# Hybrid attention and state-space layer on one core: one large load behind each of six combining steps on GpSimd, combining weights asked for five units sooner, the last gate applied to the sum

## The chip, the cores and the metric

The kernel runs on one core of a Trainium2 chip. The metric is device time in microseconds (us): the median of several executions for the kernel before, and one further execution recorded by the hardware profiler. Engines are written as in the profile: PE (TensorE matmul), PEld (its weight load), DVE (VectorE), ACT (ScalarE), POOL (GpSimd), SP (SyncE, which here only issues DMAs).

## The reference, cut to what matters

One decoder layer of 2048 tokens and width 1024. Three attention results with different dilations are merged by a softmax over their log-sum-exps, gated and normalised; a state-space branch is computed beside it; both go through one output projection and a layer norm.

```python
o1, l1 = dilated_window_attention(q, k, v, slopes, 1)
o2, l2 = dilated_window_attention(q, k, v, slopes, 4)
o3, l3 = dilated_window_attention(q, k, v, slopes, 16)
wts = softmax(stack([l1, l2, l3]), axis=0)
y_att = wts[0]*o1 + wts[1]*o2 + wts[2]*o3
y_att = rms_norm(y_att * silu(z_att), att_norm_g)
...
mix = concatenate([y_att, y_ssm])
out = mix @ w_out
x = layer_norm(alpha * x + out, ln_g, ln_b)
```

## The kernel before, in words

Up to about 1235 us of the span the kernel computes the input projection, the convolution and the state-space branch. That part is not touched. The change lies in the attention (1235 to 1727 us) and in the output projection (from 1727 us on).

**Attention.** The 16 heads are handled as 8 pairs (`pr` 0 to 7). A pair has 24 units, named by `(d, qd, half)`: three dilations `d`, four groups `qd`, two halves. Here `d` 0, 1, 2 is the dilation 16, 4, 1. The loop index `i` runs over all 192 units and three stages are in flight: at index `i` PE does the scores of unit `i`, the transposes of unit `i-2` (`TA = 2`) and the products with the values of unit `i-3`. The engines PE, DVE, ACT and POOL execute in exactly the order in which the code is written; only SP's order is chosen by the framework's scheduler. A condition such as `at == (1, 3, 0)` is tested with the unit whose values were just done, so what it guards stands three scores behind.

For a pair the tiles `q` and `k` (1 MB each, two alternating sets, so that the next pair's can be loaded while this pair runs), one `v` and, for `d` 1 and 2, a shifted `vs` (about 1 MB each) and a table `tb` per dilation are loaded. POOL issues the loads of `q`, `k`, `v`, `vs` and of the output weights `W`; it issues them in its program order, between its arithmetic. POOL also writes two permuted copies of `q` (`permute`, tile `ex`).

After a pair's last unit, `statistics(…, 1)` transposes the maxima and sums of the softmax on PE (L886), ACT copies them, SP stores them to DRAM (`d_st`), and `gather` (L906) loads them back in another layout as `cm`. Two calls of `weights` (L908) work out the three merging weights on DVE and ACT and store them (`d_wd`, L924).

**Combining.** While the next pair runs, `combine` forms the pair's merged and gated output on POOL. Each of its first three steps loads a 1 MB tile `wb`, which repeats rows of `d_wd` over 64 partitions (L937, two DMAs of 512 KB on SP), and multiplies the dilation's result `num` with it (L939); the second and third add the sum so far (L948). A fourth step multiplies by the gate `z_att` (L954) and stores the result to `d_ua` (L955). There are three `wb` slots, so the three tiles are asked for at once.

**Order before.** In the pair that runs, `weights` stands behind units `(1,1,0)` and `(1,1,1)`, the four combining steps behind `(1,3,0)`, `(2,0,0)`, `(2,1,1)`, `(2,3,0)`. `q` and `k` of the next pair are asked for at `(0,1,0)`, this pair's `v`, `vs` of `d` 2 at `(0,3,0)`, the next pair's `v` of `d` 0 at `(1,0,0)`, its `v`, `vs` of `d` 1 at `(2,1,0)`.

**Output projection.** 64 items of 24 matmuls: 16 row blocks by two branches by two halves of the columns. The first eight items use the state-space branch of four row blocks, so that the attention's last pair can be combined meanwhile, on DVE. For the last pair the gate is applied to each of the three `num` tiles beforehand (`gate`, L1071, one on POOL, two on DVE), and the third combining step writes the sum into four `PT` tiles. `split` and `squares` prepare a block, `add` merges an item into the row, `scaled` scales the residual, `norm` ends a row block.

Of the kernel before, what the change touches and what calls it, by code (L numbers as in the profile page):

```python
# [28 lines left out]
def hybrid_layer(ctx, tc, xT, xc, w52, wv, convw, convb, dtb, alog, dskp, gcol, wout,  # L29
# [669 lines left out]
    with ExitStack() as c2:  # L699
# [16 lines left out]
        def load_qk(A):  # L716
            pr = A["pr"]
            for x, src in (("q", d_q), ("k", d_k)):
                t = qk[pr % 2].tile([128, NR, NJ], F32, name=x)
                nc.gpsimd.dma_start(f2(t), src[pr])  # L720
                A[x] = {0: t} if x == "q" else t

        def load_dil(A, d):
# [5 lines left out]
            for x, o in (("v", 0),) if d == 0 else (("v", 0), ("vs", 1)):  # L729
                t = A[x][d] = io.tile([128, 16, 128], F32, name=x, bufs=3)  # L730
                if d == 0:
                    for j in range(4):
                        nc.gpsimd.dma_start(t[j:128:4], dap(d_v[0], j * D + pr * 128,
                                                            [[64 * D, 32], [4 * D, 16], [1, 128]]))
                else:
                    nc.gpsimd.dma_start(t[:, 0:16 - o], dap(d_v[d % 2], 64 * o * D + pr * 128,
                                                            [[D, 128], [128 * D, 16 - o], [1, 128]]))
# [188 lines left out]
        def combine(A, d):  # L926
# [6 lines left out]
            acc = A.get("acc")  # L933
            if d < 3:
                wb = cm_.tile([128, NR, NJ], F32, name="wb", bufs=3)
# [4 lines left out]
                if d == 2 and last:  # L940
                    for i in range(4):
                        u7.append(io.tile([128, 2, 2, 128], F32, name="PT", bufs=4).rearrange("p a b t -> p (a b) t"))
                        o7 = u7[i].rearrange("p n (r j) -> p r n j", j=8)
                        eng.tensor_tensor(o7, pv(wb)[:, :, 4 * i:4 * i + 4], pv(acc)[:, :, 4 * i:4 * i + 4],
                                          op=OP.add)
                    return
                if d:
                    eng.tensor_tensor(wb, wb, acc, op=OP.add)  # L948
                A["acc"] = wb
                return  # L950
            zt = cm_.tile([128, NR, NJ], F32, name="wb", bufs=3)
            nc.sync.dma_start(f2(zt), d_za[pr])
            u = f2(cm_.tile([128, NR, NJ], F32, name="wb", bufs=3))
            eng.tensor_tensor(pu(u), pv(acc), pv(zt), op=OP.mult)  # L954
            nc.sync.dma_start(dap(d_ua, pr * 128, [[7 * 128, 128], [128 * 7 * 128, 16], [1, 128]]),  # L955
                              u.rearrange("p (n t) -> p n t", t=128))
# [10 lines left out]
        def load_w(e, hf, name=None):  # L967
# [3 lines left out]
            s = slice(hf * 512, hf * 512 + 512)  # L971
# [97 lines left out]
        def gate(d, eng):  # L1069
            num = f2(pairs[7]["num"][d])  # L1070
            eng.tensor_tensor(num, num, zt7, op=OP.mult)  # L1071

        O = {}
        pairs = {}
        LOADS = [(8, 0, "k_0", (0, 0, 1)), (9, 0, "q_0", (0, 1, 0)), (10, 0, "ex", (0, 1, 1)), (11, 0, "vs", (0, 2, 0)),
# [7 lines left out]
        with tc.manual_schedule(engines={E.PE, E.DVE, E.Activation, E.Pool}):  # L1083
            for i in range(len(todo) + TA + 1):
                if i < len(todo):
                    pr, d, qd, half = todo[i]
                    if i == 0:
                        pairs[0] = load_pair(0)
                        load_qk(pairs[0])
                        for k in range(3):  # L1090
                            load_dil(pairs[0], k)
# [3 lines left out]
                    if (d, qd, half) == (2, 0, 0) and pr < 7:  # L1095
                        permute(pairs[pr + 1], 1)
# [6 lines left out]
                if i > TA:  # L1103
# [15 lines left out]
                    if at == (0, 1, 0) and pr < 7:  # L1119
                        load_qk(pairs[pr + 1])  # L1120
                    if pr and at == (0, 3, 0):
                        load_dil(pairs[pr], 2)
                    if pr < 7:
                        if at == (1, 0, 0):
                            load_dil(pairs[pr + 1], 0)
                        if at == (2, 1, 0):
# [146 lines left out]
```

## Time and profile before

| | us |
|---|---|
| median of 3 runs | 2137.01 |
| range of these | 2133.23 to 2138.12 |
| profiled execution, its own time | 2129.59 |
| its span in the trace | 2127.8 |
| mean granted TensorE clock | 0.969 |

The profile page gives busy time by engine and the costliest groups; the views of the trace used below are the time line of one engine (start, duration, engine, line, tiles, and in brackets the idle time before with what ended it), the chain of work that ended last, the waits, and the busy time in chosen windows. A line `SPq` is a DMA issue on SP, not the transfer. "issue" in the chain is time in which an engine waited for nothing that the trace shows.

### The profile page before, as it was taken

Reading aid. Unit: us, or ns where it says so; the run is one execution under the profiler, and the core shown is the slowest. Engines: PE = TensorE matmul, PEld = TensorE weight load, DVE = VectorE, ACT = ScalarE, POOL = GpSimd, SP = SyncE. Lnnn points to the kernel's source line nnn. Section 1 sums busy time; section 2 is a strip of 40 time slices with the busy share of each in tenths; the row PEclk is TensorE's granted clock in tenths of the full one; section 3 lists DMA queues with packets and bytes.
Section 4 is the critical chain, followed back from the end, with each engine's and each line's share of the span. In section 5 each row is a group of like instructions: output and inputs, shape, how many; then the busy total and the mean of one; then the engine's idle time right before and its main releaser. Section 6 shows DMA issues by size and latency. Waiting matters only on the chain.

```text
span 2127.8 us, 43190 instructions
## 1 busy us (share of the span) xinstructions
PE 1998.0 (94%) x16128; PEld 1626.3 (76%) x16128; DVE 1287.2 (60%) x3077; ACT 1107.9 (52%) x3045; POOL 1062.2 (50%) x877
## 2 busy tenths in 40 slices
PE   8999989989999999989999999999999868999998
PEld 7999768768777788868888867666667646888886
DVE  3441465459898556654444468777778746565453
ACT  4231445435554566646666578888788732222221
POOL 2113446657577566765555432765556771333221
PEclk9999999989999999989999999999999978999999
DMA  9999778966658777898887764777787797432310
GB/s 309 330 352 357 240 231 284 312 251 212 188 185 263 279 247 255 273 399 265 257 257 245 252 240 159 205 198 237 210 238 225 223 322 209 144 116 77 106 67 30
DMA packets 255953, 491.98 MB, mean 231 GB/s; under 512 B 43200, under 2 KB 122176, under 8 KB 244096
## 3 DMA queue, kind: packets, MB, share of 16 engines
q1 hardware_dynamic: 172096, 237.54, 35.7%
q0 software_dynamic: 40304, 168.57, 22.7%
q10 hardware_dynamic: 43344, 83.12, 12.4%
q8 instruction: 127, 2.08, 0.4%
q14 instruction: 82, 0.67, 0.1%
HBM read 333.57 MB, written 163.97 MB: 234 GB/s over the span
## 4 chain that ended last, share of the span: by engine, by line
PE 49%; DMA 7%; ACT 4%; DVE 4%; issue 2%; POOL 1%; SPq 0%; ACTq 0%; POOLq 0%; DVEq 0%
PE pp L302 6%; PE pp L306 6%; PE pp L304 6%; PE N L848 4%; PE S L1027 4%; PE S L1029 4%; PE S L795 4%; PE S L1028 3%; ACT P L807 3%; PE T L822 2%; PE T L1027 2%; PE T L1029 2%; PE T L1028 2%; DVE P L801 1%; DMA wb<-d_wd 1%
## 5 line engine op out<-in xcount | busy, mean ns | idle before, releaser
L258 POOL TENSOR_TENSOR w<-wr,w 128x512 fp32r<-128x512 f32 x231 | 345.2, 1513 | 191.7 <-ACT w L257 149.0
L807 ACT ACTIVATE P<-P,st 128x192 f32<-128x192 f32 (+1 forms) x768 | 322.0, 421 | 71.4 <-DVE st L801 67.0
L801 DVE CUSTOM_DVE_ANT_0 P<-S,tb 128x192 f32<-128x192 f32 (+1 forms) x768 | 206.9, 324 | 104.4 <-PE S L795 82.2
L311 ACT COPY ev<-pp 128x512 f32<-128x512 f32 x176 | 102.7, 583 | 249.6 <-PE pp L306 204.6
L319 DVE TENSOR_TENSOR ev<-pp,ev 128x512 f32<-128x512 f32 x152 | 101.0, 684 | 114.1 <-PE pp L306 80.9
L257 ACT CAST w<-wr 128x512 fp32r<-128x512 f32 x231 | 137.8, 618 | 40.6 <-DVE wr L250 25.4
L939 POOL TENSOR_TENSOR wb<-num,wb 128x2048 f32<-128x2048 f32 x21 | 95.5, 4549 | 125.4 <-DMA wb<-d_wd 72.2
L250 DVE TENSOR_TENSOR wr<-wr 128x512 f32<-128x512 f32 x132 | 139.6, 1058 | 11.8 <-DMA wr<-w 7.6
L807 ACT ACTIVATION_READ_ACCUMULATOR P<-P,st 128x1 f32 x768 | 144.3, 188 | 0.0
L822 PE MATMUL T<-ident,P 128*128 128x128 f32 x768 | 129.2, 291 | 10.5 <-DVE PT L824 7.4
L824 DVE COPY PT<-T 128x512 f32<-128x512 f32 x192 | 131.7, 686 | 5.6 <-PE T L822 5.3
L848 PE MATMUL N<-PT,v 128*64 128x64 f32 (+1 forms) x1536 | 126.7, 262 | 7.8 <-ACT num L878 4.4
L822 PEld LDWEIGHTS T<-ident,P 128*128 128x128 f32 x768 | 82.9, 143 | 56.8 <-issue 21.2
L402 DVE SCALAR_TENSOR_TENSOR acc<-U,cw,acc 128x2048 f32<-128x2048 f32 x36 | 122.6, 3406 | 3.6 <-ACT acc L399 3.2
L795 PE MATMUL S<-k,ex 64*64 64x192 f32 (+1 forms) x2048 | 110.9, 327 | 5.3 <-issue 5.3
L848 PEld LDWEIGHTS N<-PT,v 128*64 128x64 f32 x1536 | 79.4, 138 | 45.7 <-issue 18.7
L147 PE MATMUL pp<-vh,xh 128*128 128x256 f32 (+1 forms) x320 | 91.4, 290 | 11.5 <-ACT xh L165 10.9
L140 POOL TENSOR_TENSOR vl<-vraw,vh 128x256 fp32r<-128x256 f32 (+1 forms) x32 | 29.9, 937 | 129.0 <-ACT vh L139 121.9
L148 PE MATMUL pp<-vl,xh 128*128 128x256 f32 (+1 forms) x320 | 91.2, 289 | 0.0
L1003 DVE TENSOR_REDUCE tb<-P 128x128 f32<-128x1024 f32 x30 | 60.1, 2004 | 46.0 <-ACT P L1000 23.7
L302 PE MATMUL pp<-TT3h,w 128*128 128x512 f32 x176 | 72.7, 413 | 15.0 <-ACT ev L311 14.7
L1065 POOL TENSOR_TENSOR k<-k,wb 128x1024 f32<-128x1024 f32 x8 | 25.8, 3222 | 121.4 <-DVE k L1064 121.4
(440 smaller groups left out, 6130.7 us busy)
## 6 DMA issues: line engine op xcount, KB each, us to landing
wr<-w ACTq DMA_DIRECT2D x157, 256.0 KB
wb<-d_wd SPq DMA_DIRECT2D x48, 512.0 KB
d_wc<-w SPq DMA_DIRECT2D x44, 512.0 KB
w<-d_wc POOLq DMA_DIRECT2D x44, 512.0 KB, 5.8
csb<-d_cs ACTq DMA_DIRECT2D x32, 512.0 KB
v<-d_v POOLq DMA_DIRECT2D x16, 1024.0 KB, 10.0
st<-xT SPq DMA_DIRECT2D x31, 512.0 KB
vs<-d_v POOLq DMA_DIRECT2D x16, 960.0 KB, 11.6
```

The lines of the kernel that those rows point to most:

```text
L250: tt = lambda o, a, b, op=OP.subtract: nc.vector.tensor_tensor(q[o], q[a], q[b], op=op)
L257: nc.scalar.copy(t[:, 0], q[nm])
L258: nc.gpsimd.tensor_tensor(t[:, 1], q[nm], t[:, 0].bitcast(F32), op=OP.subtract)
L302: nc.tensor.matmul(ps, w[:, 0, k], th[:, k], start=start and k == 0, stop=False, skip_group_check=not start)
L304: nc.tensor.matmul(ps, w[:, 0, k], tl[:, k], start=False, stop=False, skip_group_check=not start)
L306: nc.tensor.matmul(ps, w[:, 1, k], th[:, k], start=False, stop=(k == 3), skip_group_check=not start)
L795: nc.tensor.matmul(o, A["q"][d][64 * h:64 * h + 64, blk, 64 * a:64 * a + 64], kv, start=True, stop=True)
L801: nc.vector.tensor_tensor_reduce(P[:, h, cs], sp[h][:, cs], t, -0.125, 3.0e38, OP.add, OP.min, accum_out=stat(A, 0, d, h, blk))
L807: nc.scalar.activation(p, p, AF.Exp, bias=stat(A, 0, d, h, blk), scale=-1.0, accum_out=stat(A, 1, d, h, blk))
L822: nc.tensor.transpose(tp[:, h, i], P[:, h, 256 * i:256 * i + 128], ident)
L824: nc.vector.tensor_copy(pt, tp)
L848: nc.tensor.matmul(o, l, r, start=start, stop=True, skip_group_check=True)
```

## The change

It splits `load_qk` and `load_dil` into loads of one tile each (`load_x`, `load_tab`, `load_v`) and the four combining steps into six: three multiplications with `wb` (`k` 0, 1, 3), two additions (2, 4), the gate (5). A table `STEPS` puts one 1 MB load behind each of them. `weights` moves to `(0,2,1)` and `(0,3,0)`. `permute` for the next pair moves to `(2,2,0)`. In pairs 6 and 7 `cm` is loaded through POOL's queue. In the last pair four output weights are loaded whole at its start, and the gate is multiplied onto the sum. In the output projection the first `add`s wait until item 2, `scaled` moves from item 0 to item 2, and the order of the weight loads changes.

```diff
-        def load_qk(A):
-            pr = A["pr"]
-            for x, src in (("q", d_q), ("k", d_k)):
-                t = qk[pr % 2].tile([128, NR, NJ], F32, name=x)
-                nc.gpsimd.dma_start(f2(t), src[pr])
+        def load_x(A, x):
+            t = qk[A["pr"] % 2].tile([128, NR, NJ], F32, name=x)
+            nc.gpsimd.dma_start(f2(t), (d_q if x == "q" else d_k)[A["pr"]])
...
-            nc.sync.dma_start(cm, dap(d_st[A["pr"]], 0, [[32, 128], [2 * S, 6], [1, 32]]))
+            (nc.sync if A["pr"] < 6 else nc.gpsimd).dma_start(cm, dap(d_st[A["pr"]], 0, [[32, 128], [2 * S, 6], [1, 32]]))
...
-        def combine(A, d):
+        def combine(A, k):
...
+            if k in (0, 1, 3):
+                d = k - k // 2
+                wb = A["wb"] = cm_.tile([128, NR, NJ], F32, name="wb", bufs=3)
                 for h in range(2):
                     nc.sync.dma_start(f2(wb[64 * h:64 * h + 64]),
                                       dap(d_wd[pr], (d * 2 + h) * S, [[0, 64], [1, S]]))
                 eng.tensor_tensor(wb, A["num"][d], wb, op=OP.mult)
...
+            elif k < 5:
+                eng.tensor_tensor(A["wb"], A["wb"], A["acc"], op=OP.add)
+                A["acc"] = A["wb"]
+            elif last:
+                for i in range(4):
...
+                    eng.tensor_tensor(u7[i].rearrange("p n (r j) -> p r n j", j=8), pv(A["acc"])[:, :, 4 * i:4 * i + 4],
+                                      pv(zt7)[:, :, 4 * i:4 * i + 4], op=OP.mult)
...
-        def gate(d, eng):
-            num = f2(pairs[7]["num"][d])
-            eng.tensor_tensor(num, num, zt7, op=OP.mult)
...
+        STEPS = {(1, 0, 0): (0, "v", 0, 2), (1, 1, 0): (1, "vs", 0, 2), (1, 2, 0): (2, "v", 1, 0),
+                 (1, 3, 0): (3, "q", 1), (2, 0, 0): (4, "k", 1), (2, 1, 0): (5, "v", 1, 1), (2, 2, 0): (None, "vs", 1, 1)}
+        LOADS = {(0, 0, 0): ((8, None, "k_0"), (9, None, "q_0"), (10, None, "ex"), (11, None, "vs")),
+                 (1, 2, 0): ((12, 0, "q_1"),), (1, 3, 0): ((13, 0, "v"),), (2, 0, 0): ((14, 0, "v"), (15, 0, "vs"))}
...
-                    if pr and at in ((1, 1, 0), (1, 1, 1)):
-                        weights(pairs[pr - 1], half)
-                    step = ((1, 3, 0), (2, 0, 0), (2, 1, 1), (2, 3, 0))
-                    if pr and at in step:
-                        combine(pairs[pr - 1], step.index(at))
+                    if pr and at in ((0, 2, 1), (0, 3, 0)):
+                        weights(pairs[pr - 1], qd - 2)
...
+                    if at in STEPS:
+                        k, x, nx, *dd = STEPS[at]
+                        if pr and k is not None:
+                            combine(pairs[pr - 1], k)
+                        if pr + nx < 8 and (pr or nx):
+                            if dd:
+                                load_v(pairs[pr + nx], x, dd[0])
+                            else:
+                                load_x(pairs[pr + nx], x)
...
-            load_w(14, 1)
-            load_w(15, 1)
+            for e in range(12, 16):
+                load_w(e, 1)
...
                 ps = product(n, br, hf)
-                if i == 0:
+                adds.append((n, br, hf, ps))
+                if i == 1:
+                    weights(A, 0)
+                    weights(A, 1)
+                if i == 2:
                     for j in range(4):
                         scaled(j)
-                if i == 1:
-                    gate(1, nc.vector)
-                    gate(2, nc.vector)
-                    weights(A, 0)
-                    weights(A, 1)
-                if i in (2, 3, 4):
-                    combine(A, i - 2)
...
+                if i > 1:
+                    while adds:
+                        add(*adds.pop(0))
+                if i == 2:
+                    combine(A, 0)
+                if i == 3:
+                    combine(A, 1)
+                    combine(A, 2)
                 if i == 4:
+                    combine(A, 3)
+                    combine(A, 4)
+                    combine(A, 5)
...
-                add(n, br, hf, ps)
```

In a row of an engine's program below stand the line, the operation, the tile written `<-` the tiles read, the shape of one operand, and a count.

POOL before, from the loads of pair 2's `q` and `k` (issued while pair 1 runs) to the gate of pair 0:

```order
L720 DMA q<-d_q_62 128x2048
L720 DMA k<-d_k_70 128x2048
L736 DMA v<-d_v_84 128x16x128
L736 DMA vs<-d_v_84 128x15x128
L733 DMA v<-d_v_84 32x16x128 x4
L760 COPY ex<-q 128x4x64 x8
L939 TENSOR_TENSOR wb<-num,wb 128x2048 x2
L948 TENSOR_TENSOR wb<-wb 128x2048
L736 DMA v<-d_v_85 128x16x128
L736 DMA vs<-d_v_85 128x15x128
L939 TENSOR_TENSOR wb<-num,wb 128x2048
L948 TENSOR_TENSOR wb<-wb 128x2048
```

POOL in the changed kernel, one pair later (pair 2 runs, pair 1 is combined, `q_63` and `k_71` belong to pair 3):

```order
L940 TENSOR_TENSOR wb<-num,wb 128x2048
L737 DMA v<-d_v_84 128x16x128
L940 TENSOR_TENSOR wb<-num,wb 128x2048
L737 DMA vs<-d_v_84 128x15x128
L944 TENSOR_TENSOR wb<-wb 128x2048
L735 DMA v<-d_v_84 32x16x128 x4
L940 TENSOR_TENSOR wb<-num,wb 128x2048
L719 DMA q<-d_q_63 128x2048
L944 TENSOR_TENSOR wb<-wb 128x2048
L719 DMA k<-d_k_71 128x2048
L955 TENSOR_TENSOR wb<-wb 128x16x16x8
L737 DMA v<-d_v_85 128x16x128
```

The next pair's `q` and `k` stood ahead of all combining of the pair; now `k` stands behind five of the six steps, and this pair's `v` and `vs` of `d` 2 (`d_v_84`) stand behind the first and the second.

DVE before, at the output projection's items 0 and 1 (`P` holds a block of the state-space branch, `num` after L1071 is the last pair's result, `cm` its statistics):

```order
L1044 SCALAR_TENSOR_TENSOR k<-S,st,k 128x512
L996 TENSOR_TENSOR ex<-P,ex 128x1024
L1003 TENSOR_REDUCE tb_20251<-P 128x128
L1038 RECIPROCAL st<-st 128x1
L1071 TENSOR_TENSOR num<-num 128x2048 x2
L913 TENSOR_TENSOR mm<-cm 128x32
```

DVE in the changed kernel at the same place:

```order
L997 TENSOR_TENSOR ex<-P,ex 128x1024
L1004 TENSOR_REDUCE tb_20241<-P 128x128
L1039 RECIPROCAL st<-st 128x1
L914 TENSOR_TENSOR mm<-cm 128x32
L915 TENSOR_TENSOR mm<-mm,cm 128x32
```

The `add` of item 0 (L1044) no longer stands ahead of the next block's `split` (L997), and the two gate multiplications ahead of the merging weights are gone.

More of the change, by code (lines that the diff above doesn't have):

```diff
@@ L728, in load_dil, with load_v @@
             nc.sync.dma_start(tb, tabs[2 * pr:2 * pr + 2, :, c0:c0 + tb.shape[2]].rearrange("h p c -> p h c"))
[L729 to L737, printed above, removed]
+        def load_v(A, x, d):
+            o, t, c0 = int(x == "vs"), io.tile([128, 16, 128], F32, name=x, bufs=3), A["pr"] * 128
+            A[x][d] = t
+            if d == 0:
+                for j in range(4):
+                    nc.gpsimd.dma_start(t[j:128:4], dap(d_v[0], j * D + c0, [[64 * D, 32], [4 * D, 16], [1, 128]]))
+            else:
+                nc.gpsimd.dma_start(t[:, 0:16 - o], dap(d_v[d % 2], 64 * o * D + c0,
+                                                        [[D, 128], [128 * D, 16 - o], [1, 128]]))
         def stat(A, k, d, h, blk):
@@ L939, in combine @@
                 eng.tensor_tensor(wb, A["num"][d], wb, op=OP.mult)
[L940 to L956, printed above, removed]
+                if k == 0:
+                    A["acc"] = wb
+            elif k < 5:
[3 more added lines that the diff above has]
+                for i in range(4):
+                    u7.append(io.tile([128, 2, 2, 128], F32, name="PT", bufs=4).rearrange("p a b t -> p (a b) t"))
+                    eng.tensor_tensor(u7[i].rearrange("p n (r j) -> p r n j", j=8), pv(A["acc"])[:, :, 4 * i:4 * i + 4],
+                                      pv(zt7)[:, :, 4 * i:4 * i + 4], op=OP.mult)
+            else:
+                zt = cm_.tile([128, NR, NJ], F32, name="wb", bufs=3)
+                nc.sync.dma_start(f2(zt), d_za[pr])
+                u = f2(cm_.tile([128, NR, NJ], F32, name="wb", bufs=3))
+                eng.tensor_tensor(pu(u), pv(A["acc"]), pv(zt), op=OP.mult)
+                nc.sync.dma_start(dap(d_ua, pr * 128, [[7 * 128, 128], [128 * 7 * 128, 16], [1, 128]]),
+                                  u.rearrange("p (n t) -> p n t", t=128))
         ring = {"ex": (io, 3), "v": (io, 3), "vs": (io, 3), "num": (cm_, 6), "wb": (cm_, 3)}
@@ L1088, in hybrid_layer @@
                         pairs[0] = load_pair(0)
-                        load_qk(pairs[0])
+                        load_x(pairs[0], "q")
+                        load_x(pairs[0], "k")
                         for k in range(3):
-                            load_dil(pairs[0], k)
+                            load_tab(pairs[0], k)
+                            load_v(pairs[0], "v", k)
+                            if k:
+                                load_v(pairs[0], "vs", k)
                         permute(pairs[0], 1)
@@ L1111, in hybrid_layer @@
                     at = d, qd, half
[L1112 to L1116 removed]
+                    if pr and at in ((0, 2, 1), (0, 3, 0)):
+                        weights(pairs[pr - 1], qd - 2)
                     if at == (0, 0, 0) and pr < 7:
                         pairs[pr + 1] = load_pair(pr + 1)
[L1119 to L1120 removed]
                     if pr and at == (0, 3, 0):
[L1122 removed]
+                        load_tab(pairs[pr], 2)
+                    if pr < 7 and at in ((1, 0, 0), (2, 1, 0)):
+                        load_tab(pairs[pr + 1], d - 1)
+                    if at in STEPS:
[5 more added lines that the diff above has]
+                                load_v(pairs[pr + nx], x, dd[0])
+                            else:
+                                load_x(pairs[pr + nx], x)
+                    if at == (2, 2, 0) and pr < 7:
+                        permute(pairs[pr + 1], 1)
                     if pr < 7:
[L1124 to L1127 removed]
                         continue
[L1129 to L1131 removed]
+                    for e, hf, name in LOADS.get(at, ()):
+                        load_w(e, hf, name)
                     if at == (2, 0, 0):
[L1133 to L1134 removed]
+                        zt7 = cm_.tile([128, NR, NJ], F32, name="num", bufs=6)
+                        nc.gpsimd.dma_start(f2(zt7), d_za[7])
                         X = big("ex", F32)
@@ L1138, in hybrid_layer @@
                         free += [big("num"), big("num")]
-                    if at in ((2, 2, 0), (2, 2, 1)):
-                        split(0, 1, slice(4 * half, 4 * half + 4))
-                    if at == (2, 3, 0):
-                        gate(0, nc.gpsimd)
+                    if at in ((2, 2, 1), (2, 3, 0)):
+                        split(0, 1, slice(4 * qd - 8, 4 * qd - 4))
             A = pairs[7]
@@ L1162, in hybrid_layer @@
             splits.update({2 * k - 5: k for k in range(10, 32)})
+            adds = []
             for i, (k, hf) in enumerate(items):
```

25 lines of the change are left out of this document (5 added, 20 removed), and 3 rows, old and new, of the table LOADS.

## Prediction

> **What bounds the kernel now.** I read the page first, then the starts of one repeated instruction for the tempo of the pairs, then the chain that ended last, then SP's and POOL's time lines.
>
> ```profile
> span 2127.8 us, 43190 instructions
> PE 1998.0 (94%) x16128; PEld 1626.3 (76%) x16128; DVE 1287.2 (60%) x3077; ACT 1107.9 (52%) x3045; POOL 1062.2 (50%) x877
> ```
>
> PE is busy 94%, POOL 50%. The change touches only the stages after 1235 us, so the average says little. The transpose of the second statistics (L886) ends each pair; its starts on PE for pairs 0, 3, 6 and 7:
>
> ```profile
> 1299.12 0.30 PE L886 MATMUL T<-ident,st 128*64 128x128 f32 x1
> 1477.36 0.30 PE L886 MATMUL T<-ident,st 128*64 128x128 f32 x1
> 1660.41 0.42 PE L886 MATMUL T<-ident,st 128*64 128x128 f32 x1
> 1727.12 0.30 PE L886 MATMUL T<-ident,st 128*64 128x128 f32 x1
> ```
>
> Pairs 1 to 6 take 1660.41 − 1299.12 = 361.3 us, 60.2 each, pair 7 66.7, and 400.7 us are left behind it. How long a pair would take without stalls shows in the chain that ended last, at the end of pair 0 and through pair 4 (start, duration, what):
>
> ```profile
> 1292.65 0.44 PE S L795 x16
> ...
> 1299.19 0.23 PE T L886
> ...
> 1515.51 0.80 PE N L848 x14
> ...
> 1526.35 0.43 PE S L795 x14
> 1526.78 2.81 issue
> 1529.59 0.58 PE S L795 x2
> ...
> 1538.84 0.23 PE T L886
> ```
>
> From the first scores of the next pair to the statistics are 1299.19 − 1292.65 = 6.5 us when nothing stalls. In pair 4 those scores (1526.35) stand 49.0 us behind the pair's start (1477.36), so a free pair takes 49.0 + 6.5 = 55.5. The 4.7 us above it in the mean pair are the stall called "issue" and what follows: in the 3 us behind it PE ran at half clock (last three columns: granted clock, DMA share, GB/s).
>
> ```profile
> 1531.00:1534.00 3.00, 3.00 (x52) 2.34 (x50) 1.02 (x2) 1.05 (x5) 2.92 (x2) 0.50 0.34 55
> ```
>
> So a free attention would save 361.3 − 6 × 55.5 = 28 us at most.
>
> **The change in a pair: POOL's chain.** Today no transfer that PE needs stands behind the combining of the same pair. In the changed order two do: `v`, `vs` of `d` 2 behind steps 0 and 1, and the next pair's `k` behind step 4. POOL works in order, so they wait for the `wb` tiles. I build that chain from pair 4 before.
>
> ```profile
> L824 DVE COPY PT<-T x6: 684/684/686, 1488.5 to 1499.4; 128x512 f32<-128x512 f32 x6
> 1500.29 0.18 DVE L913 TENSOR_TENSOR mm<-cm 128x32 f32<-128x32 f32 x1
> 1504.83 0.36 SPq L924 DMA_DIRECT2D d_wd<-cm  x1
> 1515.65 3.83 SPq L937 DMA_DIRECT2D wb<-d_wd  x6
> 1325.92 0.36 SPq L924 DMA_DIRECT2D d_wd<-cm  x1
> ...
> 1327.75 3.68 SPq L937 DMA_DIRECT2D wb<-d_wd  x6
> 1523.18 4.56 POOL L939 TENSOR_TENSOR wb<-num,wb 128x2048 f32<-128x2048 f32 x1 [17.78 <-ACT P L807]
> 1529.35 4.52 POOL L939 TENSOR_TENSOR wb<-num,wb 128x2048 f32<-128x2048 f32 x1 [1.60 <-DMA wb<-d_wd]
> 1533.95 4.54 POOL L948 TENSOR_TENSOR wb<-wb 128x2048 f32<-128x2048 f32 x1
> 1538.43 1.20 POOL L736 DMA_DIRECT2D v<-d_v  x1
> 1434.98 1.32 POOL L733 DMA_DIRECT2D v<-d_v  x2
> 1431.48 0.60 POOL L720 DMA_DIRECT2D q<-d_q  x1
> k<-d_k POOLq DMA_DIRECT2D x1, 1024.0 KB, 5.1
> ```
>
> Counted from the pair's start (1477.36):
> - The weights begin on DVE at 1500.29, that is +22.9. Six `PT` copies start between 1488.5 and 1499.4, so five units take 10.9 there; the changed kernel begins at +12.0. `cm` has to be there by then; in pair 4 it was asked for at about +12, because the burst of loads delayed it. In the new order the burst is gone by then, so I cost this at nothing; it costs what `cm` is late.
> - Weights to the store of `d_wd`: 1504.83 − 1500.29 = 4.5, so +16.6. This is DVE work that only moves, from units bound by PE to units bound by ACT: between 0 and 1 us a pair gained or lost, taken as 0.
> - Store to the `wb` loads: 10.8 in pair 4, with 5 MB of other loads in flight, 1.83 in pair 1 without. The new order has none in flight: +18.4. Behind SP's `d_wd` nothing now waits for the table `tb`.
> - First `wb` to its multiplication: 1523.18 − 1515.65 = 7.5, +25.9. Step 0 takes 4.56: +30.5; `v` is issued in 1.2. The second `wb` allows 1529.35 − 1515.65 = 13.7, +32.1. Step 1: +36.6; `vs` 1.2; step 2 (4.54): +42.4; `v` of the next pair, four pieces, 2.6: +45.0; step 3: +49.6; `q` 0.6; step 4: +54.7.
> - Only then `k` is issued. A 1 MB load with nothing beside it lands 5.1 us after its issue (last row): **+59.8**.
>
> PE wants `k` for the first scores of the next pair at +49.0: it is 10.8 us late. The `vs` of `d` 2 lands at 36.6 + 5.1 = +41.7, while the first products of `d` 2 stand at 1515.51, +38.2: 3.5 us late, but this stall lies inside the wait for `k` that follows. The old "issue" stall disappears in it too. From `k` on, the pair needs 6.5 us if PE keeps its clock; after the stall of pair 4 it needed 1538.84 − 1529.59 = 9.3 with nearly all first scores done, 9.9 with them. A pair thus takes 66.3 to 69.7, and I take 68.0 because the 2.81 us stall already cost clock: 6 × 68.0 − 361.3 = **+46.7** (+36 to +57). Everything behind `k` (step 5, `v`, `vs` of `d` 1, permuting: some 12 us of POOL) ends near +67, when the next pair starts, so it adds nothing to the period.
>
> [...]
>
> **Pair 7.** Here four whole output weights (4 MB) are issued at its start, so the `d_wd` store is held again:
>
> ```profile
> SPq L937 <- DMA d_wd<-cm: 7.9, 1, 7.9
> ```
>
> With 7.9 in place of 1.83 the `wb` loads are issued at +24.5, the second multiplication ends at 24.5 + 13.7 + 4.5 = 42.7, and `vs` lands at +47.8 against +38.2: 9.6 late, and 3 of slow clock. The pair takes 55.5 + 12.6 = 68 against 66.7: **+1.4** (−4 to +6).
>
> **The output projection.** A row block is four items:
>
> ```profile
> 1963.09 3.34 POOL L1065 TENSOR_TENSOR k<-k,wb 128x1024 f32<-128x1024 f32 x1 [17.01 <-DVE k L1064]
> ...
> 1985.82 3.34 POOL L1065 TENSOR_TENSOR k<-k,wb 128x1024 f32<-128x1024 f32 x1 [16.90 <-DVE k L1064]
> ...
> 2100.00:2127.00 27.00, 18.50 (x82) 14.74 (x80) 7.71 (x14) 0.82 (x3) 4.25 (x2) 0.93 0.10 39
> ```
>
> 22.73 us for four, 363.7 for 64; PE ends at 2118.5. From 1727.1 that leaves 2118.5 − 1727.1 − 363.7 = 27.7 us lost. The chain that ended last says where:
>
> ```profile
> 1744.96 7.44 DMA ex<-xc
> ...
> 1758.88 4.39 DVE num L1071 x2
> 1763.27 0.11 DVE mm L913
> ...
> 1770.49 8.11 DMA wb<-d_wd
> ...
> 1780.47 2.30 DVE wb L939
> ```
>
> The residual's arrival holds `scaled` (L1010) on ACT, with it item 0's `add` and the `split` behind it on DVE, then the gates (4.4 us), and only at 1763 the weights. In the new order the `split` of block 2 waits for no residual, the gates are gone and the weights can begin when `cm` lands, some 17 us sooner. What is late next: the second halves of weights 12 to 15 are issued behind `cm` on POOL, some 15 us behind the start, and land about 7 us later, while item 3 wants them after three items, 17 us: 5 us and some slow clock; and block 3's `split` stands behind two combining steps: 2 to 3 us. The multiplications on DVE are five passes and the gate, where they were two gates, four passes and the sum; POOL loses one gate (it had time). I leave 13.7 us lost of 27.7: **−14** (0 to −22).
>
> **Sum.** 46.7 + 1.4 − 14 = +34 us. On the profiled execution's own 2129.6 this gives 2164; the median of the runs is 7.4 above that execution (2137.0), and a median for the changed kernel is likewise put at 2171.
>
> **Rivals.**
> - *The chain doesn't reach PE* (faster). It decides at one point: `k` has to land before +49.0, 10.8 us sooner than my sum. Then pairs cost 55.5 + 0.5, 6 × 56 − 361.3 = −25, and with −14 and +1 the median is 2099. Against it: five POOL passes of 4.5 with the issues between (1.2, 1.2, 2.6, 0.6) and one landing of 5.1 are 33.4 us that no load order shortens, and they begin behind weights that begin at +12.0. Even with `wb` loads that cost nothing it would come at 18.4 + 33.4 = +51.8. For it: only weights far earlier than +12.0. 5%.
> - *Broadcast loads at the rate of the others.* If the `wb` bursts are slow only because of what lies beside them, the first lands after 5.1, at +23.5, and POOL alone sets the rest: step 4 ends at 23.5 + 5 × 4.5 + 5.6 = +51.6, `k` lands at +56.7, a pair takes 63.2 to 66.6, say 65: 6 × 65 − 361.3 = +29, in all +16, 2153. [...] Against it: the spread of 7.5 and 13.7 was measured when only these loads were in flight. 10%.
> - *The output projection gives back all of its loss, the pairs near their low end*: +30 − 24 and pair 7 −4: +2, no change, 2139. The chain's rows allow it if weights 12 to 15 land in time. 8%.
> - *`cm` is late as well.* SP issues the `d_ua` store ahead of the statistics' stores, and that waits for step 5; if this closes into a ring, a pair takes 72: +71 + 1 − 14 = +58, 2195. 8%.
>
> **How the numbers follow.** My forecast, the chain at 66 to 70 us a pair, has 69%; its own range is 2150 to 2192. The range for 8 in 10 takes in the second rival, the edge of the third and part of the fourth: 2140 to 2196. A difference of 0.2% (4.3 us) is about what a measurement of this kernel can tell from no change. Faster by more: the first rival and a little of the third, 7%. Within it, the rest of the third: 6%. Slower: 87%.
>
> **What would show it.** In the profile after: PE's scores (L796) waiting for the DMA `k<-d_k` at the start of pairs 2 to 7, some 3 to 8 us each; PE's products waiting for `vs<-d_v` at the start of `d` 2; starts of the second statistics 66 to 70 us apart; the first POOL multiplication about 26 us behind a pair's start with little idle time between the steps; no "issue" stall of the old kind that counts. Wrong would be: starts 56 to 60 us apart (the loads were in time after all), the first multiplication before +22 (the broadcast was cheaper), waits for `cm` on DVE at the new place of the weights (the fourth rival), or a projection that still takes 400 us behind the last statistics.

## The result, and the profile after

| | before | after |
|---|---|---|
| median, us | 2135.12 (4 runs, 2127.86 to 2138.12) | 2156.51 (4 runs, 2153.76 to 2159.33) |
| ratio, 95% interval | | 1.0105 [1.0075, 1.0135] |
| profiled execution: span, us | 2127.8 | 2152.0 |
| mean granted TensorE clock | 0.969 | 0.965 |

The changed kernel is 21 us slower; 2171 was predicted, with a range of 2140 to 2196. One execution of run e3 below (3816 us, where the other three took 2164 to 2173) was in a slower state and is left out of that run's median and ratio. The lines of the code have moved by one: L796 is the scores, L849 the products with the values, L887 the transpose of the second statistics, L907 `cm`, L914 the first instruction of the weights, L938 and L940 the load of `wb` and its multiplication.

The starts of the second statistics on PE, for pairs 0, 3, 4, 6 and 7 of the changed kernel:

```profile
1291.62 0.30 PE L887 MATMUL T<-ident,st 128*64 128x128 f32 x1
1495.49 0.30 PE L887 MATMUL T<-ident,st 128*64 128x128 f32 x1
1565.10 0.30 PE L887 MATMUL T<-ident,st 128*64 128x128 f32 x1
1700.14 0.30 PE L887 MATMUL T<-ident,st 128*64 128x128 f32 x1
1764.93 0.30 PE L887 MATMUL T<-ident,st 128*64 128x128 f32 x1
```

They cut the span into four parts, which the tables below use throughout. Pairs 1 to 6 are 1700.14 − 1291.62 = 408.5 us, 68.1 each.

| us | to the end of pair 0 | pairs 1 to 6 | pair 7 | behind it |
|---|---|---|---|---|
| before | 1299.1 | 361.3 | 66.7 | 400.7 |
| after | 1291.6 | 408.5 | 64.8 | 387.1 |
| difference | −7.5 | +47.2 | −1.9 | −13.6 |
| predicted | 0 | +46.7 | +1.4 | −14 |

What PE waited for between 1290 and 1765 us (us in total, times, longest; cut to the rows used below), before and then after:

```profile
PE S L795 <- issue: 14.2, 6, 3.4
...
PE N L848 <- DMA vs<-d_v: 3.5, 2, 3.2
```

```profile
PE S L796 <- DMA k<-d_k: 36.1, 6, 6.7
PE N L849 <- issue: 10.5, 6, 3.0
...
PE S L796 <- issue: 5.8, 3, 2.7
PE N L849 <- DMA vs<-d_v: 4.0, 3, 2.5
```

A wait that was not there before, six times some 6 us, is for `k` of the next pair. It ends only the last part of a pair, so the rows ahead of it matter: here is the chain in one pair, POOL's time line after the change (in brackets the idle time before, and what ended it), then SP's and DVE's rows for its beginning.

```profile
1521.19 4.55 POOL L940 TENSOR_TENSOR wb<-num,wb 128x2048 f32<-128x2048 f32 x1 [27.56 <-DMA wb<-d_wd]
1525.69 1.20 POOL L737 DMA_DIRECT2D v<-d_v  x1
1526.91 4.54 POOL L940 TENSOR_TENSOR wb<-num,wb 128x2048 f32<-128x2048 f32 x1
...
1544.24 0.60 POOL L719 DMA_DIRECT2D q<-d_q  x1
1544.87 4.57 POOL L944 TENSOR_TENSOR wb<-wb 128x2048 f32<-128x2048 f32 x1
1549.36 0.58 POOL L719 DMA_DIRECT2D k<-d_k  x1
```

```profile
1500.72 0.38 SPq L907 DMA_DIRECT2D cm<-d_st  x1
...
1510.72 0.36 SPq L925 DMA_DIRECT2D d_wd<-cm  x1
1512.39 5.10 SPq L938 DMA_DIRECT2D wb<-d_wd  x6
```

```profile
1507.25 0.18 DVE L914 TENSOR_TENSOR mm<-cm 128x32 f32<-128x32 f32 x1
```

POOL stands idle for 27.56 us, and from then on it works without a gap: five passes of 4.55 us with a load behind each. The chain of work that ended last closes it, and it says that PE's first scores of the next pair were released by the transfer:

```profile
1544.87 4.50 POOL wb L944
1549.36 6.09 DMA k<-d_k
...
1555.59 1.13 PE S L796 x16
```

### The profile page after: what moved, and what is told of

Same layout as the page of the kernel before. It is cut to its first block, busy times and chain, and to the rows that moved or that the text cites. A ratio compares the mean times of both kernels' runs of the same rounds, so it can differ in the third digit from the quotient of the medians.

```text
span 2152.0 us, 43174 instructions
## 1 busy us (share of the span) xinstructions
PE 2003.5 (93%) x16128; PEld 1632.9 (76%) x16128; DVE 1280.1 (59%) x3076; ACT 1107.9 (51%) x3045; POOL 1062.5 (49%) x874
## 4 chain that ended last, share of the span: by engine, by line
PE 46%; DMA 8%; ACT 5%; POOL 5%; DVE 3%; issue 2%; SPq 0%; ACTq 0%; POOLq 0%; DVEq 0%
PE pp L302 6%; PE pp L306 6%; PE pp L304 6%; PE S L1028 3%; PE S L1030 3%; PE S L1029 3%; PE N L849 3%; ACT P L808 3%; POOL wb L940 3%; PE S L796 3%; PE T L823 2%; DMA wb<-d_wd 2%; DMA k<-d_k 2%; PE T L1028 2%; PE T L1029 2%
## 5 line engine op out<-in xcount | busy, mean ns | idle before, releaser
L258 POOL TENSOR_TENSOR w<-wr,w 128x512 fp32r<-128x512 f32 x231 | 352.4, 1544 | 176.3 <-ACT w L257 128.5
L940 POOL TENSOR_TENSOR wb<-num,wb 128x2048 f32<-128x2048 f32 x21 | 95.5, 4549 | 193.6 <-DMA wb<-d_wd 165.2
L250 DVE TENSOR_TENSOR wr<-wr 128x512 f32<-128x512 f32 x132 | 150.8, 1142 | 15.6 <-DMA wr<-w 12.2
L849 PE MATMUL N<-PT,v 128*64 128x64 f32 (+1 forms) x1536 | 128.7, 263 | 17.8 <-ACT num L873 7.5
L849 PEld LDWEIGHTS N<-PT,v 128*64 128x64 f32 x1536 | 80.8, 140 | 56.9 <-issue 26.6
L796 PE MATMUL S<-k,ex 64*64 64x192 f32 (+1 forms) x2048 | 113.4, 331 | 5.8 <-issue 5.8
L402 DVE SCALAR_TENSOR_TENSOR acc<-U,cw,acc 128x2048 f32<-128x2048 f32 x36 | 114.4, 3176 | 2.4 <-ACT acc L399 2.0
L147 PE MATMUL pp<-vh,xh 128*128 128x256 f32 (+1 forms) x320 | 91.6, 291 | 10.8 <-ACT xh L165 10.8
```

The lines of the kernel that those rows point to most:

```text
L250: tt = lambda o, a, b, op=OP.subtract: nc.vector.tensor_tensor(q[o], q[a], q[b], op=op)
L258: nc.gpsimd.tensor_tensor(t[:, 1], q[nm], t[:, 0].bitcast(F32), op=OP.subtract)
L796: nc.tensor.matmul(o, A["q"][d][64 * h:64 * h + 64, blk, 64 * a:64 * a + 64], kv, start=True, stop=True)
L849: nc.tensor.matmul(o, l, r, start=start, stop=True, skip_group_check=True)
L940: eng.tensor_tensor(wb, A["num"][d], wb, op=OP.mult)
```

## The experiments

Two statements were to be tested: the pair is bound by `k`'s place at the end of POOL's chain (the prediction), and this place is all that is wrong with the new order. The runs came in four groups (e1 to e4, e5 to e8, e9 to e11, e12), each beside the kernel before on its own chip (medians 2126.9, 2129.0, 2131.4 and 2129.9 us, 7 to 19 runs); between groups the ratios are to be compared, not the times. The parts are from one profile of each.

| run | median, us | ratio, 95% interval | to end of pair 0 | pairs 1 to 6 | pair 7 | behind |
|---|---|---|---|---|---|---|
| e1 q, k early | 2151.2 | 1.0114 [1.0086, 1.0143] | 1298.1 | 396.3 | 72.1 | 384.9 |
| e2 v, vs of d 2 early | 2146.6 | 1.0096 [1.0066, 1.0125] | 1292.2 | 409.9 | 60.0 | 386.4 |
| e3 both early | 2169.0 | 1.0189 [1.0147, 1.0231] | 1305.8 | 415.9 | 64.5 | 385.2 |
| e4 weights two units later | 2184.4 | 1.0279 [1.0246, 1.0311] | 1291.8 | 438.1 | 67.1 | 384.4 |
| e5 old pairs, new end | 2124.7 | 0.9971 [0.9953, 0.9989] | 1297.5 | 360.8 | 76.8 | 388.2 |
| e6 two loads behind a step | 2111.5 | 0.9914 [0.9881, 0.9947] | 1293.5 | 366.3 | 63.5 | 385.8 |
| e7 other rows | 2154.4 | 1.0121 [1.0089, 1.0152] | 1296.1 | 407.9 | 64.5 | 383.7 |
| e8 k two steps sooner | 2125.2 | 0.9992 [0.9973, 1.0010] | 1288.8 | 370.5 | 71.9 | 384.4 |
| e9 far rows | 2129.2 | 0.9988 [0.9972, 1.0005] | 1293.7 | 376.6 | 71.6 | 379.8 |
| e10 third read later | 2119.5 | 0.9945 [0.9926, 0.9965] | 1293.9 | 370.5 | 71.2 | 384.8 |
| e11 and last pair | 2116.8 | 0.9931 [0.9914, 0.9948] | 1295.1 | 368.0 | 62.7 | 390.9 |
| e12 one read each | 2515.2 | 1.1811 [1.1765, 1.1857] | 1297.5 | 663.3 | 117.1 | 439.2 |

**e1 to e3: the loads back to their early places, the weights where the change put them.**

```diff
-        STEPS = {(1, 0, 0): (0, "v", 0, 2), (1, 1, 0): (1, "vs", 0, 2), (1, 2, 0): (2, "v", 1, 0),
-                 (1, 3, 0): (3, "q", 1), (2, 0, 0): (4, "k", 1), ...
+        STEPS = {(1, 0, 0): (0, "v", 0, 2), (1, 1, 0): (1, "vs", 0, 2), (1, 2, 0): (2, "v", 1, 0),
+                 (1, 3, 0): (3, None, 0), (2, 0, 0): (4, None, 0), ...
...
+                    if at == (0, 1, 0) and pr < 7:
+                        load_x(pairs[pr + 1], "q")
+                        load_x(pairs[pr + 1], "k")
```

e2 does the same with `v` and `vs` of `d` 2, at `(0,3,0)`; e3 does both.

> The changed kernel, with the next pair's q and k asked for at (0,1,0) again, ahead of all combining steps; everything else as changed. Theory (k behind POOL's fifth combining pass sets the pair's length): the six waits of PE's first scores for k go; what is late next is vs of d 2 behind step 1, some 2 to 4 us a pair, with slow clock. Pairs 1 to 6 fall from 408 us to about 366 (61 each), the time from 2156 to about 2114. Rival (loads spread among the broadcasts cost by contention, or the earlier weights cost, wherever k stands): pairs stay at 66 to 68 us, time 2145 to 2156.

> The changed kernel, with this pair's v and vs of d 2 asked for at (0,3,0) again, q and k left behind steps 3 and 4. Theory: the small waits for vs go, but k still arrives at the same time or later, since two more MB are in flight when the weights are stored and hold that store by up to 8 us; pairs 68 to 74 us, time 2150 to 2190. Rival (vs is what costs): pairs fall by 4 us or more, time 2130 or less.

> The changed kernel, with q, k, and v, vs of d 2 all asked for ahead of the combining steps; weights, six steps and the changed output projection kept. Theory: no transfer that PE needs soon stands behind the combining; pairs take 56 to 60 us, what is left above 55.5 is the old issue stall; pairs 1 to 6 together 336 to 360 against 361 before and 408 changed; with the output projection's 14 us the time is 2085 to 2120, faster than both kernels. Rival (contention): pairs stay above 64 us, time above 2130.

In e1 the wait for `k` is gone, as expected, and yet pairs 1 to 6 take 396.3 us: the time lies in the range of the rival, and so does e3's. The waits of DVE and PE in e1 name what took its place, POOL's, SP's and DVE's rows of its pair 3 (which begins at 1424.47) say why:

```profile
DVE mm L914 <- DMA cm<-d_st: 37.0, 6, 8.3
PE N L849 <- DVE PT L825: 33.3, 6, 7.8
```

```profile
1422.06 1.20 POOL L737 DMA_DIRECT2D v<-d_v  x1
1423.25 1.20 POOL L737 DMA_DIRECT2D vs<-d_v  x1
...
1429.40 0.59 POOL L719 DMA_DIRECT2D q<-d_q  x1
1429.99 0.55 POOL L719 DMA_DIRECT2D k<-d_k  x1
```

```profile
1425.78 2.85 SPq L901 DMA_DIRECT2D d_st<-sT  x4
1441.52 0.38 SPq L907 DMA_DIRECT2D cm<-d_st  x1
```

```profile
1443.76 0.19 DVE L914 TENSOR_TENSOR mm<-cm 128x32 f32<-128x32 f32 x1 [7.36 <-DMA cm<-d_st]
```

POOL finishes the combining of the pair before, and then nothing holds it: it issues four loads of about 1 MB within 9 us, a position in the code notwithstanding. The statistics' small stores are issued among them: from 1435.5 to 1438.5, while SP waits for them, POOL's loads took 95.9% of the time of the 16 DMA engines, and 162 small packets of SP's queue 3.0%. `cm` can be asked for only when the stores have landed: 1441.52 − 1424.47 = 17.1 us into the pair, where the changed kernel asked at 1500.72 − 1495.49 = 5.2. SP's wait for these stores between 1300 and 1760 us, in e1 and in the changed kernel:

```profile
SPq L907 <- DMA d_st<-sT: 62.5, 9, 12.7
```

```profile
SPq L907 <- DMA d_st<-sT: 7.9, 8, 2.9
```

The weights, now placed at +12, make DVE wait, in order, and with it the transposes' copies and PE. My expectation for e1 and e3 overlooked this; it is the fourth rival of the prediction, with another cause than the one named there (a burst of loads, not SP's store of the gated sum). e2 keeps `k` at the end of the chain and adds the burst as well: PE waits 24.1 us for `k` and 11.3 behind DVE, and the pairs stay at 409.9 us, 68.3 each, as the theory had it; the time, 2146.6, is 3 us below its range. e3 has all four loads early, no wait for `k`, and PE waits longest behind DVE:

```profile
PE N L849 <- DVE PT L825: 57.5, 6, 12.4
```

So the second statement falls: `cm`, which the early weights need, came soon where the DMA engines had little to do while the statistics were stored (the changed kernel, whose loads are spread: a share of 0.07 to 0.39 between 1497 and 1501), and late where a burst took 95.9% of their time (e1).

**e4: the weights two units later, all else as changed.**

```diff
-                    if pr and at in ((0, 2, 1), (0, 3, 0)):
-                        weights(pairs[pr - 1], qd - 2)
+                    if pr and at in ((0, 3, 1), (1, 0, 0)):
+                        weights(pairs[pr - 1], d)
```

> The changed kernel, with the merging weights asked for two units later. Theory (one chain from the weights on DVE to the landing of k): each of the six pairs grows by those two units, 4 to 5.5 us, pairs 72 to 74, time 2180 to 2190. Rival (POOL or the loads are late for another reason than the weights): less than 1.5 us a pair, time below 2166.

The pairs take 438.1 − 408.5 = 29.6 us more, 4.9 each. Two units were 2 × (10.9 / 5) = 4.4 us in the prediction's rows. The delay at the head of the chain passed through it whole.

**e5: the order of before in the pairs, the new end.** `weights` back at `(1,1,0)`, `(1,1,1)`, the steps at their four old places, the loads early; whole-row loads in pair 7, the gate on the sum and the late `add`s stay.

```diff
+        STEPS = {(0, 1, 0): ((), ((1, "q"), (1, "k"))), (0, 3, 0): ((), ((0, "v", 2), (0, "vs", 2))),
+                 (1, 0, 0): ((), ((1, "v", 0),)), (1, 3, 0): ((0,), ()), (2, 0, 0): ((1, 2), ()),
+                 (2, 1, 0): ((), ((1, "v", 1), (1, "vs", 1))), (2, 1, 1): ((3, 4), ()), (2, 3, 0): ((5,), ())}
```

> The pairs go back to the order of before (q and k of the next pair asked for at (0,1,0), v and vs of dilation 2 at (0,3,0), weights at (1,1,0) and (1,1,1), the six steps at the four old places), and only the end is that of the change: whole-row loads at the start of pair 7, the gate on the sum, the sums behind the products. Theory of the prediction (the projection gives 14 us, the pairs take 47): the pairs are those of before, 60 to 61 us each, and the time is before's less 12 to 15 us, 2111 to 2116 beside a before of 2127. Rival (the projection was shorter only because the late pairs gave its loads more time): 2122 to 2128.

The pairs are those of before (360.8 against 361.3), and the part behind pair 7 keeps its gain: 388.2 − 400.7 = −12.5. The time, 2124.7, is in the rival's range all the same, because pair 7 takes 76.8 in place of 66.7; and since a longer pair 7 gives the projection's loads more time, e5 alone doesn't rule the rival out. The other runs do: in e2 and e6 pair 7 takes 60.0 and 63.5, less than before, and the part behind it is 14.3 and 14.9 shorter. In pair 7 of e5 the new end doesn't suit the old pairs: `cm` of pair 6 goes through POOL's queue, behind the late combining of pair 5, and the four whole weights are issued on its heels. Which of these costs the 10 us wasn't tested.

```profile
1672.84 4.54 POOL L955 TENSOR_TENSOR wb<-wb 128x2048 f32<-128x2048 f32 x1
1677.34 0.87 POOL L907 DMA_DIRECT2D cm<-d_st  x1
1678.20 0.57 POOL L973 DMA_DIRECT2D k<-d_wo  x1
```

**e8 and e6: `k` sooner, the loads still behind POOL's steps.** e8 exchanges two loads:

```diff
-        STEPS = {..., (1, 2, 0): (2, "v", 1, 0), (1, 3, 0): (3, "q", 1), (2, 0, 0): (4, "k", 1), ...
+        STEPS = {..., (1, 2, 0): (2, "k", 1), (1, 3, 0): (3, "q", 1), (2, 0, 0): (4, "v", 1, 0), ...
```

> Of the changed kernel only two loads change places: k of the next pair is asked for behind step 2 and v of dilation 0 behind step 4. Theory (PE waits for the last of q and k at the end of the chain): k lands some 12 us sooner and q, behind step 3, is now the last, 5 us late, so pairs of 62 to 64 us and 2115 to 2125 us. Rival (the pair is bound by the chain on GpSimd as a whole or by cm): no change, 2148 to 2160 us.

Pairs of 370.5 / 6 = 61.8 us, 6.3 shorter than in the changed kernel; the wait for `k` is gone, and the wait for `q` that I expected in its place is 0.2 us in all. That one exchange takes back 38 of the 47 us, and so shows the first statement. Its pair 7 took 71.9 us, with one wait of 6.8 us for `v` in it, whose cause stays open.

e6 asks for all loads sooner, several behind a step:

```diff
+        STEPS = {(1, 0, 0): ((0,), ((0, "v", 2), (0, "vs", 2))), (1, 1, 0): ((1,), ((1, "k"), (1, "q"))),
+                 (1, 2, 0): ((2,), ((1, "v", 0),)), (1, 3, 0): ((3,), ((1, "v", 1), (1, "vs", 1))),
+                 (2, 0, 0): ((4,), ()), (2, 1, 0): ((5,), ())}
```

> The weights stay where the change put them, the loads stay behind steps on GpSimd but more than one of them behind a step, so that they are asked for sooner: v and vs of dilation 2 behind step 0, k and q behind step 1, v of dilation 0 behind step 2, v and vs of dilation 1 behind step 3, none behind steps 4 and 5. Theory (k was late by its place in the chain, and the combining weights by quiet queues): k lands about 43 us into the pair, before PE wants it at 49, the queues are quiet when the statistics are stored, pairs of 58 to 61 us, 2104 to 2118 us. Rival (with short pairs the store of the gated sum and the last loads run into the statistics of the next pair, and cm is late as in the run with q and k early): pairs of 64 to 68 us, DVE waits for cm, 2137 to 2155 us.

Pairs of 61.1 us and a median of 2111.5, the fastest of all, 0.9% below before. What PE still waits for in e6, between the end of pair 0 and 1659.8:

```profile
PE N L849 <- issue: 10.9, 7, 3.0
PE S L796 <- issue: 9.5, 5, 2.8
PE N L849 <- ACT num L873: 6.4, 6, 1.2
PE N L849 <- DMA vs<-d_v: 2.3, 3, 1.1
```

No `k`, no `cm`. The "issue" stalls, 20.4 us, are now the largest. Pairs 1 to 6 are still 5 us longer than before (366.3 against 361.3): even the best placing of the new order that was tried gains nothing in the pairs, and its lead comes from the end (−14.9) and pair 7 (−3.2).

**e7, e9, e12: what makes the loads of `wb` slow.** The changed kernel's queues in 8 us in which only these loads run (packets, MB, time of the packets as a share of the 16 DMA engines' time; q1 takes what SP issues, q0 what POOL issues), and e1's in 3 us with `q` and `k`, whose packets are as large:

```profile
q1 hardware_dynamic: 258, 1.72, 101.6%
```

```profile
q0 software_dynamic: 163, 1.20, 95.9%
```

1.72 MB in 8 us are 215 GB/s, and with 8 KB a packet 1.016 × 16 × 8 / (1.72 MB / 8192 B) = 0.62 us each. `q` and `k` move at 400 GB/s, 0.31 us a packet. e7 reads other rows of the small array, e9 rows that lie 8 KB apart in the gate's array; in both the values multiplied are not the combining weights.

```diff
-                                      dap(d_wd[pr], (d * 2 + h) * S, [[0, 64], [1, S]]))
+                                      dap(d_wd[pr], min((d * 2 + h) * S, 8224), [[32, 64], [1, S]]))   # e7
+                                      dap(d_za[pr], h * 64 * S, [[S, 64], [1, S]]))                    # e9
```

> Each load of the combining weights reads 64 different stretches of 8 KB, 128 B apart, in place of one stretch 64 times; bytes, packets and destinations are the same, the weights that arrive are those of other positions. Theory (the packets are slow, about 0.62 us, since all read the same row, and this holds the chain back): packets of about 0.31 us, the first multiplication about 3 us sooner and the third no longer waiting, k about 5 us sooner, pairs of 62 to 64 us, 2118 to 2128 us. Rival (the 8 KB packets are slow by their number or their place, not by the row): no change from the changed kernel, 2148 to 2160 us.

> The changed kernel, but the loads of the combining weights read 64 rows of the 1 MB gate array (rows 8 KB apart, each once) in place of one row of the 48 KB weight array 64 times; bytes, packets and destinations are the same, the weights that arrive are the gate's, and the loads wait no longer for the store of the weights, only for their turn on SP behind it. Theory A (the packets are slow because they all read one small place; 128 B apart was no other place): 0.31 us a packet, the first multiplication about 4 us sooner, the k wait down to 0 to 2 us a pair and q the last, pairs of 62 to 64 us, 2115 to 2130 us. Theory B (such loads are slow by their number, three times 1 MB at once, wherever they read): still 0.6 us a packet, only the 2 us of the store saved in each pair, pairs of 66 to 67 us, 2138 to 2150 us.

e7 is the changed kernel again, in time and in its packets (1.71 MB in 8 us). e9's time fell where theory A put it, but not for A's reason. Its loads wait for no store of the weights: SP issued them 28.6 us ahead of the end of the pair whose result they multiply (1481.98), where the changed kernel issues them 16.9 us behind it. The head of the chain is gone:

```profile
1453.38 6.87 SPq L938 DMA_DIRECT2D wb<-d_za  x6
```

and its packets are still slow. Over 4 us of e9 (1648 to 1652) with these loads and a few small stores, and over 2 us of the kernel before (1478 to 1480) with the load of the gate for the fourth combining step:

```profile
q1 hardware_dynamic: 130, 0.86, 99.2%
```

```profile
q1 hardware_dynamic: 98, 0.80, 98.7%
```

The first is 215 GB/s and 0.992 × 16 × 4 / (0.86 MB / 8192 B) = 0.60 us a packet, the second 401 GB/s and 0.32 us. So it is not the row that is read 64 times. Nor is it SP's queue or the array: both rows are loads of 8 KB rows of the gate's arrays, issued by SP. Nor is it the number of bytes at once: e1's burst of four loads ran at 400 GB/s. What is left is that each load at 215 GB/s goes to one half of the partitions, and each at 400 GB/s to all; the former are also of 512 KB and the latter of 1 MB, and no run here changes one without the other, so which of the two makes the rate wasn't shown.

e12 was meant to load the combining weights at full width:

```diff
-                for h in range(2):
-                    nc.sync.dma_start(f2(wb[64 * h:64 * h + 64]),
-                                      dap(d_wd[pr], (d * 2 + h) * S, [[0, 64], [1, S]]))
+                nc.sync.dma_start(f2(wb), dap(d_wd[pr], d * 2 * S, [[S, 2], [0, 64], [1, S]]))
```

> The kernel with several loads behind a step (2111.5 us, pairs of 61.1 us), and each combining weight is loaded by one DMA into all 128 partitions in place of two, one into the lower 64 partitions and one into the upper 64; what is loaded is the same. Theory A (the 8 KB packets take 0.6 us because each such load goes to 64 partitions only, whatever it reads: q, k and the gate go to 128 and take 0.31 to 0.39): 0.31 to 0.40 us a packet, 3 MB of them in 8 to 10 us in place of 15, the gaps 14 to 15 units into the pair gone, pairs of 57.5 to 60 us, 2090 to 2105 us. Theory B (3 MB of them at once are slow, however they are cut): still about 0.6 us, pairs of 60 to 62 us, 2105 to 2117 us.

Both theories missed, by 400 us. Over 18 us of e12 with this load alone:

```profile
q1 hardware_dynamic: 119, 0.96, 12.7%
```

12.7% of the time of 16 engines is that of two: 0.96 MB took these 18 us, 53 GB/s, and from 1300 to 1760 PE waited 85.6 us for `v`, 43.7 for `q` and 27.7 for `vs`, which POOL issues behind steps that wait for such loads. Why no more than two were at work in the mean wasn't shown. A packet took 0.127 × 16 × 18 / (0.96 MB / 8192 B) = 0.31 us, so an 8 KB packet of the weights isn't slow by itself; it was slow, 0.62 us, in the loads into 64 partitions, with all 16 engines at work (101.6%). As a dose, e12 agrees with the chain: later `wb` tiles, pairs of 111 us.

**e10 and e11: the third `wb` load behind `v` and `vs`.** On the base of e6; e11 also asks for pair 7's `v` and `vs` of `d` 2 at `(0,3,0)`.

```diff
-                for h in range(2):
-                    nc.sync.dma_start(f2(wb[64 * h:64 * h + 64]),
-                                      dap(d_wd[pr], (d * 2 + h) * S, [[0, 64], [1, S]]))
+                for i in (d,) if last or k == 0 else (1, 2) if k == 1 else ():
...
+                        (nc.gpsimd if i == 2 and not last else nc.sync).dma_start(
+                            f2(wb[64 * h:64 * h + 64]), dap(d_wd[pr], (i * 2 + h) * S, [[0, 64], [1, S]]))
```

> The kernel with several loads behind a step, and the load of the third combining weights is taken from SP's queue, where it runs together with the first two, to GpSimd's, behind the loads of v and vs of dilation 2. Theory (in its pairs v and vs of dilation 2 and PE's own instructions stand behind 3 MB of these loads, which is where 3 to 4 us a pair are left): the gap 14 to 15 units into the pair goes, pairs of 57.5 to 60 us, 2094 to 2106 us. Rival (the order within the same bytes gives nothing, or k and q are now late behind the third load): 2108 to 2125 us.

> The run before with one thing more: in the last pair v and vs of dilation 2 are asked for at (0,3,0), as in the run with both of them early, where that pair took 60.0 us beside 63.5. Theory: 3 us less than the run before. Rival: no difference, since what is saved in pair 7 is waited for in the projection.

e10 misses its theory (2119.5 against 2094 to 2106) and falls to the rival. The "issue" stalls at the start of `d` 2 fall, but PE waits for `vs` instead, three units later; e10's waits from 1300 to 1760:

```profile
PE N L849 <- DMA vs<-d_v: 20.6, 7, 4.8
...
PE N L849 <- issue: 6.5, 8, 1.7
```

The same bytes in another order move the stall, they don't remove it. e11 saves 8.5 us in pair 7 against e10 and gives 6.1 back behind it, as its rival says. Its median is 2.8 us lower, about the 3 of its theory, but the runs of the two overlap (2114.5 to 2122.2 and 2114.1 to 2118.6), so the times don't decide.

## Why the prediction was right, and where it was not

**The chain in the pairs: right, row by row.** In pair 4, which begins at 1495.49:

| us from the pair's start | predicted | after |
|---|---|---|
| weights begin | 12.0 | 11.8 |
| store of `d_wd` | 16.6 | 15.2 |
| loads of `wb` | 18.4 | 16.9 |
| first multiplication | 25.9 | 25.7 |
| second | 32.1 | 31.4 |
| PE ready for the next pair's first scores | 49.0 | 53.4 |
| `k` issued | 54.7 | 53.9 |
| `k` landed | 59.8 | 60.0 |
| length of a pair, mean | 68.0 | 68.1 |

Two sizes were off and cancelled, which is luck: the head of the chain was 1.5 us faster than forecast, the first `wb` took 8.8 in place of 7.5 (the row from which 7.5 was read names ACT, not the load, as what ended that wait).

**The free pair of 55.5 us: not reached.** PE was ready for the first scores at 1555.59 − 6.73 = 1548.86, that is +53.4, so it waited 6.7 us for `k` where the sum has 10.8. The length of the pair didn't suffer, since the landing of `k` sets it. But the shortest of the pairs 1 to 7 in any run here is 58.3 us (e5), and e6, with no wait for `k` or `cm`, has 61.1 in the mean. So no run bears out the free pair, nor the first rival's 56 us, which is built on it.

e4 and e8 show from both sides that the chain sets the pair: 4.9 us a pair more with a later head, 6.3 less with `k` two steps sooner.

**"The burst is gone by then, so I cost this at nothing; it costs what `cm` is late": right for this kernel**, with `cm` asked for at +5.2. e1 and e3 show the price once the burst is back: DVE waits 37 us for `cm` in e1. It is the point at which a remedy that the prediction's chain alone suggests (early loads) goes wrong.

**"The old issue stall disappears": wrong, at no cost here.** PE has 10.5 + 5.8 us of it after. It lies at the start of `d` 2, at the time of the 3 MB of `wb` loads, ahead of the wait for `k`, which takes it in. What makes it isn't shown. In e6, without that wait, it is the largest stall of the pairs.

**`vs` 3.5 us late, hidden in the wait for `k`: the right sign, a smaller size** (1.5 us in pairs 1 to 6 together, in two of them).

**Pair 7: wrong in sign, small.** The term was +1.4 and measured −1.9. The step that failed is the 7.9 us put for the held store, which was read in pair 4: the `wb` loads were issued 1720.58 − 1715.36 = 5.2 us behind it. The first multiplication came 1728.31 − 1700.14 = 28.2 us behind the pair's start (32.0 by that step), and `vs` was 2.5 us late, not 9.6.

**The output projection: right.** The weights begin 17.0 us behind the end of pair 7, 36.1 before; 19 us sooner, where some 17 were forecast:

```profile
1781.94 0.19 DVE L914 TENSOR_TENSOR mm<-cm 128x32 f32<-128x32 f32 x1 [3.92 <-DMA cm<-d_st]
```

The part is −14 against −13.6, and −12.5 to −20.9 in the experiments, but for e11 (−9.8, behind a shorter pair 7) and e12 (its `wb` loads are slow there too). "What is late next" was about right in sum, 8.9 us against 7 to 8, but not in its parts: PE waits behind pair 7 for block 3's `split` 6.5 us, where 2 to 3 were forecast, and for a weight 2.4, where 5 were, and not for numbers 12 to 15 but for one of the eight that are asked for last (`num`):

```profile
PE S L1030 <- DVE num L997: 6.5, 1, 6.5
PE S L1028 <- DMA num<-d_wo: 2.4, 1, 2.4
```

**The sum.** The three parts touched add 47.2 − 1.9 − 13.6 = +31.7, where +34 was predicted; the medians differ by 21.4. The part to the end of pair 0 was 7.5 us shorter in the one profile of after than in the one of before, and all of it lies ahead of the attention: PE's first scores begin at 1228.1 after and 1235.6 before, and from there to the end of pair 0 both take 63.5. In the twelve experiments pair 0 ends between 1288.8 and 1305.8. So a difference of that size between two executions is scatter; whether a few microseconds of it are real isn't settled, with one profile of before. Together, 31.7 − 7.5 = 24.2 us is the difference of the two profiled executions.

**The rivals.** The second (loads of `wb` at the others' rate) predicted 2153, nearer to the median than my forecast, and is still wrong: the loads ran at 215 GB/s against 400. A time alone would have picked it. The first would have needed `k` by +49. The third fell with pairs of 68 us; its own sum was also off, since it takes +30 for the pairs where the low end of the prediction's range is +36, and −24 for all of a loss of 27.7. The fourth didn't happen in the changed kernel and did in e1 and e3.

## What to carry to other kernels

POOL, which here issues loads between its arithmetic, ran as far ahead as its waits let it: loads that nothing held were issued four within 9 us, wherever they stood in the code (e1), and `k`, behind the fifth step, came at +53.9, at the end of the whole chain ahead of that step (after). So look up two numbers for each load: when it may start without holding up small transfers on which the next stage depends, and when its reader wants it. Here e6, with the same steps and the same loads put between these two, turned +1.1% into −0.9%; and a gain in one part (the end, 14 us) should be sought apart from the reordering that came with it, which gained nothing in the pairs.

## What the runs showed of the hardware that wasn't expected

- Loads of 8 KB rows into 64 partitions at a time ran at 215 GB/s with 0.60 to 0.62 us a packet (after, e7, e9, each with other rows read), against 400 GB/s and 0.31 to 0.32 us into 128 (e1 in POOL's queue, the gate before in SP's).
- One load of 1 MB into 128 partitions in place of two of 512 KB into 64 each (e12) took 12.7% of the time of the 16 DMA engines, that of two: 0.96 MB in 18 us.
- The statistics' four stores at the end of a pair, 8 KB each, held back `cm` by 12 us when four loads of about 1 MB were issued around them (e1: asked for at +17.1, after: +5.2).
